# Two fused transformer blocks on one core: final norms placed by hand, the residual added by accumulating transfers, a two-part compression product

## The chip, the cores and the metric

The kernel runs on one core of one Trainium2 chip, as one launch. The metric is the device time of one execution in microseconds (us). The number given for the kernel before is the median of three runs; a fourth run was profiled, and every row of a trace below comes from that one execution. A change counts as measurable here from about 0.2% on.

## The reference, cut to what matters

Two blocks over 512 tokens of width 2048, in float32. The first is a gated block (linear recurrence beside latent attention), which the change doesn't touch. Of the second, this is what it touches:

```python
def compress(kv, pe, w1, w2):            # keys and values for the compressed attention
    ch = kv.reshape(b, s // 16, 16, g, d)                  # b=1, s=512, g=4, d=64
    blocks = jnp.concatenate([ch[:, r:nc + r] for r in range(2)], axis=2)   # 32 long, stride 16
    blocks = blocks + pe[None, None, :, None, :]
    hid = jax.nn.silu(jnp.einsum('bnlgd,lde->bnge', blocks, w1))
    return jnp.einsum('bnge,ef->bngf', hid, w2)

def second_block(x, p, ...):
    ...
    x = x + merged @ w_out                                              # x2 below
    x = x + jax.nn.sigmoid(x @ w_ple_gate) * (p @ w_ple)                # gated product
    return rms_norm_2(x, final_g)                                       # x * rsqrt(mean(x^2) + eps) * final_g
```

## The kernel before

**Precision.** TensorE's operands are float32 values split into two float32r parts, hi and lo (`split`: ScalarE rounds to hi, VectorE subtracts to get lo), and a product is three matmuls, hi·hi, hi·lo and lo·hi (`mm3`).

**Order.** The program is one stream. `spine` is a list of units, each with a weight tile (fetched on the SP queue, split ahead of use) and a generator of matmuls. Everything that isn't spine work is a generator in `sides`. After each step of a unit, `pump` advances those generators whose awaited tiles are known to be ready by `Clock`, a planner that adds up assumed durations for each engine and for transfers; `until` and `drain` advance them regardless, the one whose tiles are ready first going first. What comes out is a fixed order for each engine: an instruction that waits holds all that stand behind it on its engine. Intermediate tiles of 128x512 come from one pool of 78 slots (`slot`), and a transfer into a slot waits until the slot's last reader is done.

**Compression** (`compress`, once for keys, once for values, while the spine does the input product of the second block). For each of four groups `c`, VectorE adds the position term into `a`, a 128x(4x128) tile; ScalarE rounds it to `cAh`, VectorE subtracts to get `cAl`; then 8 matmuls of 128 columns go into `hid`, alternating between `cAh` and `cAl` with the same weights `w1`, whose 128 columns hold the hi and lo parts of 64 outputs. So there are 2 x 4 x 8 = 64 matmuls.

**The gate product** x2 @ w_ple_gate runs as Strassen's seven products on 256-token halves (`PROD`, in the order 1, 7, 6, 2, 5, 3, 4), for two pairs of 512-column quarters (p = 0, 1). The operand sums are the `F` tiles; those of products 5 and 3 are made by `late_forms` while the product of pair 0 runs. Output tile (b, c) is token block b (of 128 tokens) and column quarter c. Product 2 completes tiles (0, 2p) and (1, 2p), product 5 (2, 2p+1) and (3, 2p+1), product 3 (0, 2p+1) and (1, 2p+1), product 4 (2, 2p) and (3, 2p). So with p = 1, the last tile of blocks 0 and 1 comes from product 3, and that of blocks 2 and 3 from product 4, which is the last.

**The gated sum** (`gated`). `gate_load` brings two tiles from DRAM by POOL's queue: p @ w_ple (`plel`, stored early in the program) and x2 (`x3`, called x in the trace). Then ScalarE: tanh(src/2); VectorE (`stt`): t = (t + 1) * plel; VectorE (`stt`): x = 0.5 t + x; ScalarE: square of x with a row sum into `ssq`; and a multiplication by the norm's gain on VectorE for some tiles. The tiles of quarter c = 0, 1 get their gain later (`first_gains`).

**The end** (`last_product`, `finish`). The last product is cut by token block: block 2 first (tile j = 0, 512 columns), then block 3 in two halves of 256 columns (24 matmuls each). After each part its gated sum is emitted at once. `finish(b)` then sums the four row sums, takes the reciprocal root in nine small VectorE instructions, scales the four tiles (three or two on ScalarE, the rest on VectorE) and sends four transfers of 256 KB to the output, on SP, ACT, SP and POOL's queues. `finish(0)` and `finish(1)` wait as generators and are emitted, with the others, in `drain` after the last matmul.

Of the kernel before, what the change touches and what calls it, by code (L numbers as in the profile page):

```python
# [9 lines left out]
F32R = mybir.dt.float32r  # L10
I32 = mybir.dt.int32
AF = mybir.ActivationFunctionType
OP = mybir.AluOpType
# [3 lines left out]
D = 2048  # L17
# [226 lines left out]
def emit(ctx, tc, I, out):  # L244
    nc = tc.nc
    V, A, T, G, Q = nc.vector, nc.scalar, nc.tensor, nc.gpsimd, nc.sync
# [6 lines left out]
    clock = Clock()  # L253

    def slot(shape, name, dt=F32):
        return sp.tile(shape, dt, name=name, tag="s", padded_shape=None)
# [7 lines left out]
    def small(name, n=16):  # L264
        return mp.tile([128, n], F32, name=name, tag="m")
# [4 lines left out]
    def f(ap):  # L270
        return ap.bitcast(F32)
# [10 lines left out]
    def tt(o, a, b, op):  # L282
        V.tensor_tensor(o, a, b, op=op)  # L283
        clock.note("V", 0.07 + size(o) * 1.04e-3, [o], [a, b])
# [16 lines left out]
    def stt(o, a, s, b, op0, op1, **k):  # L301
        V.scalar_tensor_tensor(o, a, s, b, op0=op0, op1=op1, **k)  # L302
        clock.note("V", 0.07 + per_lane(s) + size(o) * 1.04e-3, [o, *k.values()], [a, s, b])
# [9 lines left out]
    def act(o, a, fn=AF.Identity, **k):  # L313
        A.activation(o, a, fn, **k)  # L314
        n = sum(isinstance(x, bass.AP) for x in k.values())
        clock.note("A", (0.05 if psum(a) else 0.095) + 0.093 * n + size(a) * 0.835e-3,
                   [o] + ([k["accum_out"]] if "accum_out" in k else []), [a, *k.values()])

    def mm(o, l, r, start, stop_, on=False):

        T.matmul(o, l, r, start=start, stop=stop_, skip_group_check=on)  # L321
        clock.note("PE", max(0.107, size(r) * (0.419e-3 if r.dtype == F32R else 1.67e-3)), [o], [l, r])
# [5 lines left out]
    def dma(q, o, a):  # L328
        {"Q": Q, "A": A, "G": G}[q].dma_start(o, a)
        clock.dma(q, o, a)  # L330
# [9 lines left out]
    def mm3(o, lh, ll, rh, rl, start=False, stop_=False, on=False):  # L340
        mm(o, lh, rh, start, False, on)
        mm(o, lh, rl, False, False, on)
        mm(o, ll, rh, False, stop_, on)
# [57 lines left out]
    sides = Sides(clock, WIDTH)  # L401
# [38 lines left out]
    def ple_unit(c):  # L440
        def mmf(hi, lo):
            for b in range(TB):
                ps = bank("pple")
                t = slice(b * 128, (b + 1) * 128)
                for kk in range(2):
                    mm3(ps, pTh[kk][:, t], pTl[kk][:, t], hi[:, kk, :], lo[:, kk, :], kk == 0, kk == 1)
                squares((XK + (KT,) * 16)[4 * c + b])
                o = slot([128, 512], "pleo")
                act(o, ps, AF.Copy)
                stores.append((ple_d[b][c], o))  # L450
                first_group(4 * c + b - RB)
                yield

        return Unit(block("w_ple_2", 0, 2, (c * 512, (c + 1) * 512)), (2, 512), mmf)
# [342 lines left out]
    kl0, kl1, _ = PARTS[0][-1]  # L797
# [616 lines left out]
    oa_d = [dram(f"oa{i}") for i in range(8)]  # L1414
    sg_d = [dram(f"sg{i}") for i in range(32)]
    c1 = 0.7978845608028654
    done = {"oa": [], "ob": [], "sg": [], "x2": 0, "c22": 0}

    def gelu2_gen(x, **k):

# [162 lines left out]
    def compress(kind):  # L1583
# [4 lines left out]
        w1 = []  # L1588
        w1v = w1_.rearrange("(l q) d e -> (q d) l e", q=2)
        w1r = []  # L1590
        for half in range(2):
            w = slot([128, 8, 64], "w1r")
# [5 lines left out]
        for g in range(4):  # L1598
            e = slot([128, 264], "E")
            V.memset(e[:, 256:264], 0.0)  # L1600
            src = kc_[kind, g // 2][(g % 2) * 64:(g % 2 + 1) * 64]
# [9 lines left out]
        for q in range(4):  # L1611
            w = slot([128, 4, 128], "w1s", F32R)
            src = w1r[q // 2][:, (q % 2) * 4:(q % 2) * 4 + 4, :]
# [8 lines left out]
        hid = bank("phid")  # L1622
        for c in range(4):
            a = slot([128, 4, 128], "cA")
            o, r0 = c // 2, (c % 2) * 4
            for g in range(4):
                ev = E[g].rearrange("p (n r) -> p r n", r=8)
                tt(a[:, :, g * 32:(g + 1) * 32], ev[:, r0:r0 + 4, o:o + 32],
                   pec[:, 4 * c:4 * c + 4, None].to_broadcast([128, 4, 32]), OP.add)
            ah, al = slot([128, 4, 128], "cAh", F32R), slot([128, 4, 128], "cAl", F32R)  # L1630
            yield [a]
            act(ah, a, AF.Copy)
            yield [ah]
            tt(al, a, f(ah), OP.subtract)
            yield [al]
            for l in range(4):
                mm(hid[:, :128], w1[c][:, l, :], ah[:, l, :], c == 0 and l == 0, False)
                mm(hid[:, :128], w1[c][:, l, :], al[:, l, :], False, c == 3 and l == 3)
        yield [hid]
        hs, th = slot([64, 128], "hs"), slot([64, 128], "th")  # L1640
        act(th, hid[64:128, :128], AF.Copy)
        yield [th]
        tt(hs, hid[:64, :128], th, OP.add)
        yield [hs]
        act(th, hs, AF.Tanh, scale=0.5)
        yield [th]
# [287 lines left out]
    sg = {}  # L1934
# [62 lines left out]
    x2_d = dram("x2t", (128, TB, D))  # L1997
    x2r, F = {}, {}
# [120 lines left out]
    x3, pl_, acc, tmp, part = {}, {}, {}, {}, {}  # L2119

    def gate_load(b, c):
        x3[b, c] = slot([128, 512], "x3")
        pl_[b, c] = slot([128, 512], "plel")
        dma("G", pl_[b, c], ple_d[b][c])
        dma("G", x3[b, c], x2_d[:, b, c * 512:(c + 1) * 512])

    def gated(b, c, src, s=slice(0, 512), end=None):

        yield [src, x3[b, c], pl_[b, c]]
        x = x3[b, c][:, s]  # L2130
        t = slot([128, 512], "tgate")[:, s]
        act(t, src, AF.Tanh, scale=0.5)
        yield [t]
        stt(t, t, 1.0, pl_[b, c][:, s], OP.add, OP.mult)
        stt(x, t, 0.5, x, OP.mult, OP.add)
        if end is not None:
            stt(t, x, 1.0, x, OP.mult, OP.mult, accum_out=end)
            return
        yield [x]
        act(t, x, AF.Square, accum_out=ssq[:, b, c:c + 1])  # L2140
        if c > 1 and (b < 2 or c == 3):
            tt(x, x, pl_["fg", c], OP.mult)
        pl_.pop((b, c))
        nsum[b] += 1
        if b < 2 and nsum[b] == 4:
            yield [ssq]
            sides.spawn(finish(b, ()))
        if b > 1 and nsum[b] == 3:
            sides.spawn(part_gen(b))

# [2 lines left out]
    def first_gains():  # L2153
        for c in range(2):
            for b in range(TB):
                yield [x3[b, c]]
                tt(x3[b, c], x3[b, c], pl_["fg", c], OP.mult)
        done["gains"] = True
# [39 lines left out]
    def from_4(j, c):  # L2198
        t, ps = tmp.pop(("w", j)), acc.pop(("e", j))
        yield [t, ps]  # L2200
        tt(t, ps, t, OP.subtract)
        yield from gated(2 + j, c, t)
# [59 lines left out]
        return [mk(u) for u in range(4)]  # L2262

    def last_product(u, ws):
        def part_(j, ks, s, end):
            ps = acc["e", j][:, s]
            for k in ks:
                hi, lo = ws[k // 2]
                w, t = F["4", k], slice(j * 128, (j + 1) * 128)
                mm3(ps, w[:, 0, t], w[:, 1, t], hi[:, k % 2, s], lo[:, k % 2, s], False, k == 7, True)  # L2270
                yield
            if end is not None:
                x = tmp["w", j][:, s]
                tt(x, ps, x, OP.subtract)
                for _ in gated(2 + j, 2, x, s, end):
                    pass

        e0 = small("sqe")
        yield from part_(0, (2 * u, 2 * u + 1), slice(0, 512), e0[:, 0:1] if u == 3 else None)
        if u == 3:  # L2280
            sides.spawn(finish(2, (e0[:, 0:1],)))
            e1, e2 = small("sqe"), small("sqe")
            yield from part_(1, range(8), slice(0, 256), e1[:, 0:1])
            yield from part_(1, range(8), slice(256, 512), e2[:, 0:1])
            sides.spawn(finish(3, (e1[:, 0:1], e2[:, 0:1])))

    def part_gen(b):
        yield [ssq]
# [2 lines left out]
        tt(p[:, 0:1], p[:, 0:1], ssq[:, b, 3:4], OP.add)  # L2291
        ts(p[:, 0:1], p[:, 0:1], 1.0 / D, EPS, OP.mult, OP.add)

    def finish(b, sums):

        while "gains" not in done:
            yield
        yield
        if sums:
            ms = part[b]  # L2300
            for o in sums:
                stt(ms[:, 0:1], o, 1.0 / D, ms[:, 0:1], OP.mult, OP.add)
        else:
            ms = part[b] = small("part")
            reduce(ms[:, 0:1], ssq[:, b, :], OP.add)
            ts(ms[:, 0:1], ms[:, 0:1], 1.0 / D, EPS, OP.mult, OP.add)
        r = rsqrt1(ms)
        yield
        for n, c in enumerate((2, 3, 1, 0)):
            y = x3[b, c]  # L2310
            if sums and c == 2:
                stt(y, y, r, pl_["fg", c], OP.mult, OP.mult)
            elif n < 3:
                act(y, y, AF.Identity, scale=r)
            else:
                ts(y, y, r, None, OP.mult)
            dma("QAQG"[n], out[0, b * 128:(b + 1) * 128, c * 512:(c + 1) * 512], y)

    def rsqrt1(ms):

# [115 lines left out]
```

## Time and profile before

| | |
|---|---|
| median of 3 runs | 2384.18 us (2383.25 to 2385.69) |
| the profiled execution | 2384.71 us, its span in the trace 2382.8 us |
| TensorE (PE) busy | 2339.3 us, 98% of the span, 11323 matmuls |
| VectorE (DVE) busy | 1534.0 us, 64% |
| ScalarE (ACT) busy | 974.7 us, 41% |
| GpSimd (POOL) busy | 291.9 us, 12% |
| mean granted TensorE clock | 0.995 of full speed |
| moved by transfers | 383.10 MB, mean 161 GB/s |

Times in rows are in us from the start of the span, durations in us unless marked ns. PE's weight loads (PEld) overlap its matmuls, and a matmul's printed duration is longer than the distance to the next one, since they are pipelined: the pace is read from the starts. On DVE and ACT too the next instruction can start some tenths of a us before the printed end of the one before. "Idle before" is the time that an engine waited, with what released it.

### The profile page before, as it was taken

Reading aid. Unit: us, or ns where it says so; the run is one execution under the profiler, and the core shown is the slowest. Engines: PE = TensorE matmul, PEld = TensorE weight load, DVE = VectorE, ACT = ScalarE, POOL = GpSimd, SP = SyncE. Lnnn points to the kernel's source line nnn. Section 1 sums busy time; section 2 is a strip of 40 time slices with the busy share of each in tenths; the row PEclk is TensorE's granted clock in tenths of the full one; section 3 lists DMA queues with packets and bytes.
Section 4 is the critical chain, followed back from the end, with each engine's and each line's share of the span. In section 5 each row is a group of like instructions: output and inputs, shape, how many; then the busy total and the mean of one; then the engine's idle time right before and its main releaser. Section 6 shows DMA issues by size and latency. Waiting matters only on the chain.

```text
span 2382.8 us, 30848 instructions
## 1 busy us (share of the span) xinstructions
PE 2339.3 (98%) x11323; PEld 1960.3 (82%) x11323; DVE 1534.0 (64%) x2918; ACT 974.7 (41%) x1791; POOL 291.9 (12%) x432
## 2 busy tenths in 40 slices
PE   8999999999999999999999999999999999999996
PEld 6778889888888988888888888888888888888785
DVE  6777988788866357558888437877233445333777
ACT  6423265655533343335444224544223222222554
POOL 0000030342212002000010100000111200110120
PEclk9999999999999999999999999999999999999998
DMA  9986732333355354624444634444545633444684
GB/s 344 350 271 239 256 129 72 124 122 105 111 177 185 97 160 139 185 89 124 130 127 142 172 98 124 125 110 128 144 148 178 216 111 111 140 134 133 234 300 150
DMA packets 124167, 383.10 MB, mean 161 GB/s; under 512 B 16542, under 2 KB 16836, under 8 KB 123504
## 3 DMA queue, kind: packets, MB, share of 16 engines
q1 hardware_dynamic: 94896, 273.41, 35.1%
q0 software_dynamic: 28256, 106.58, 15.0%
q8 instruction: 89, 1.46, 0.2%
q10 hardware_dynamic: 864, 1.14, 0.1%
q14 instruction: 62, 0.51, 0.1%
HBM read 343.32 MB, written 71.30 MB: 174 GB/s over the span
## 4 chain that ended last, share of the span: by engine, by line
PE 58%; DVE 3%; issue 1%; ACT 1%; DMA 1%; POOL 0%; ACTq 0%; DVEq 0%; POOLq 0%
PE pch L321 46%; PE pgb L321 2%; PE pO L321 2%; PE psc L321 2%; PE pge L321 2%; PE pPT L325 1%; DVE wlo L283 1%; PE pgc L321 1%; PE pga L321 0%; ACT whi L314 0%; DVE cA L283 0%; PE pcs L321 0%; PE px L325 0%; DMA w1r<-in_cmp_w_v_dram 0%; DVE vx L302 0%
## 5 line engine op out<-in xcount | busy, mean ns | idle before, releaser
L283 DVE TENSOR_TENSOR wlo<-wraw,whi 128x1024 fp32r<-128x1024 f32 (+5 forms) x421 | 497.5, 1182 | 191.7 <-ACT whi L314 189.5
L314 ACT ACTIVATE whi<-wraw 128x1024 fp32r<-128x1024 f32 (+5 forms) x423 | 425.1, 1013 | 318.8 <-PE pch L321 118.9
L321 PE MATMUL pch<-h2h,whi 128*128 128x512 f32 x1216 | 483.2, 397 | 0.0
L321 PE MATMUL pch<-h2h,wlo 128*128 128x512 f32 x1216 | 474.9, 391 | 0.0
L321 PE MATMUL pch<-h2l,whi 128*128 128x512 f32 x1216 | 474.5, 390 | 0.0
L321 PEld LDWEIGHTS pch<-h2h,wlo 128*128 128x128 f32 x1216 | 228.2, 188 | 48.9
L321 PEld LDWEIGHTS pch<-h2l,whi 128*128 128x128 f32 x1216 | 228.8, 188 | 40.7
L321 PEld LDWEIGHTS pch<-h2h,whi 128*128 128x128 f32 x1216 | 228.6, 188 | 41.0
L314 ACT ACTIVATE P<-psc,sm 128x512 f32<-128x512 f32 (+3 forms) x160 | 83.7, 527 | 134.2 <-DVE sm L306 103.9
L321 PE MATMUL pp<-hh,whi 128*128 128x512 f32 x320 | 126.1, 394 | 0.2 <-DVE acc L283 0.2
L321 PE MATMUL pp<-hh,wlo 128*128 128x512 f32 x320 | 124.7, 390 | 0.0
L321 PE MATMUL pp<-hl,whi 128*128 128x512 f32 x320 | 124.6, 389 | 0.0
L321 PE MATMUL pch<-mgh,whi 128*128 128x512 f32 x256 | 101.1, 395 | 0.0
L321 PE MATMUL pch<-mgh,wlo 128*128 128x512 f32 x256 | 99.9, 390 | 0.0
L321 PE MATMUL pch<-mgl,whi 128*128 128x512 f32 x256 | 99.6, 389 | 0.0
L321 PE MATMUL pch<-oh,whi 128*128 128x512 f32 x256 | 99.6, 389 | 0.0
L321 PE MATMUL pch<-ol,whi 128*128 128x512 f32 x256 | 99.6, 389 | 0.0
L321 PE MATMUL pch<-oh,wlo 128*128 128x512 f32 x256 | 99.6, 389 | 0.0
L283 DVE TENSOR_TENSOR mg<-pch,R 128x512 f32<-128x512 f32 x32 | 22.1, 690 | 116.4 <-PE pch L321 116.4
L314 ACT ACTIVATE PTh<-pPT 128x512 fp32r<-128x512 f32 (+1 forms) x120 | 59.6, 529 | 90.7 <-PE pPT L325 88.3
L306 DVE TENSOR_REDUCE sm<-psc 128x1 f32<-128x512 f32 (+3 forms) x160 | 78.6, 491 | 5.5
L283 DVE TENSOR_TENSOR PTl<-pPT,PTh 128x512 fp32r<-128x512 f32 (+1 forms) x120 | 68.1, 594 | 9.8 <-ACT PTh L314 9.6
(538 smaller groups left out, 4755.6 us busy)
## 6 DMA issues: line engine op xcount, KB each, us to landing
wraw<-in_w_in_dram SPq DMA_DIRECT2D x199, 512.0 KB, 3.6
wada<-in_w_mod_dram SPq DMA_DIRECT2D x128, 256.0 KB, 5.4
wraw<-in_w_out_dram SPq DMA_DIRECT2D x64, 512.0 KB, 3.5
wgate<-in_w_gate_dram SPq DMA_DIRECT2D x64, 256.0 KB, 4.8
wraw<-in_w_ple_gate_dram SPq DMA_DIRECT2D x24, 512.0 KB, 4.2
ws0x<-in_w_ple_gate_dram POOLq DMA_DIRECT2D x16, 512.0 KB, 7.8
ws1x<-in_w_ple_gate_dram POOLq DMA_DIRECT2D x16, 512.0 KB, 6.2
sg<-mg POOLq DMA_DIRECT2D x32, 256.0 KB, 2.6
```

Source lines behind the costliest of these rows:

```text
L283: V.tensor_tensor(o, a, b, op=op)
L306: V.tensor_reduce(o, a, AX.X, op, **k)
L314: A.activation(o, a, fn, **k)
L321: T.matmul(o, l, r, start=start, stop=stop_, skip_group_check=on)
L325: T.transpose(o, a, i)
```

## The change

It does three things.

1. Compression: `cAh` and `cAl` of two of the four rows of `a` now lie side by side in one tile `cA2`, so that one matmul of 256 columns takes both parts: 32 matmuls instead of 64. The rounding and the subtraction go in halves of 256 columns (two of each per group instead of one), and at the end the two halves of `hid` are added with one more ScalarE copy and two more VectorE additions.
2. The residual: p @ w_ple is stored with a factor 0.5. For 14 of the 16 tiles x2 is no longer loaded ahead; VectorE makes (t + 1) * plel in place, and a transfer from DRAM on POOL's queue with an accumulate adds x2 to it. The square, and all behind it, waits for that transfer. Tiles (2, 2) and (3, 2) keep the load of x2 and an addition on VectorE.
3. The end: the last product has no halves any more (24 matmuls of 512 columns for block 3). Before the gated sum of block 2 is emitted, `until` emits `finish(0)` and `finish(1)` to their end; `finish(2)` is emitted behind block 2's gated sum, ahead of block 3's matmuls in the program, and block 3's sum and `finish(3)` follow.

```diff
@@ -446,7 +446,7 @@
                     mm3(ps, pTh[kk][:, t], pTl[kk][:, t], hi[:, kk, :], lo[:, kk, :], kk == 0, kk == 1)
                 squares((XK + (KT,) * 16)[4 * c + b])
                 o = slot([128, 512], "pleo")
-                act(o, ps, AF.Copy)
+                act(o, ps, AF.Copy, scale=0.5)
                 stores.append((ple_d[b][c], o))
                 first_group(4 * c + b - RB)
                 yield
@@ -1414,7 +1414,7 @@
     oa_d = [dram(f"oa{i}") for i in range(8)]
     sg_d = [dram(f"sg{i}") for i in range(32)]
     c1 = 0.7978845608028654
-    done = {"oa": [], "ob": [], "sg": [], "x2": 0, "c22": 0}
+    done = {"oa": [], "ob": [], "sg": [], "x2": 0, "c22": 0, "out": 0}
 
     def gelu2_gen(x, **k):
 
@@ -1627,20 +1627,25 @@
                 ev = E[g].rearrange("p (n r) -> p r n", r=8)
                 tt(a[:, :, g * 32:(g + 1) * 32], ev[:, r0:r0 + 4, o:o + 32],
                    pec[:, 4 * c:4 * c + 4, None].to_broadcast([128, 4, 32]), OP.add)
-            ah, al = slot([128, 4, 128], "cAh", F32R), slot([128, 4, 128], "cAl", F32R)
-            yield [a]
-            act(ah, a, AF.Copy)
-            yield [ah]
-            tt(al, a, f(ah), OP.subtract)
-            yield [al]
-            for l in range(4):
-                mm(hid[:, :128], w1[c][:, l, :], ah[:, l, :], c == 0 and l == 0, False)
-                mm(hid[:, :128], w1[c][:, l, :], al[:, l, :], False, c == 3 and l == 3)
+            for half in range(2):
+                w = slot([128, 2, 2, 128], "cA2", F32R)
+                src = a[:, 2 * half:2 * half + 2]
+                yield [a]
+                act(w[:, :, 0], src, AF.Copy)
+                yield [w]
+                tt(w[:, :, 1], src, f(w[:, :, 0]), OP.subtract)
+                yield [w]
+                for l in range(2):
+                    n = 4 * c + 2 * half + l
+                    mm(hid[:, :256], w1[c][:, 2 * half + l, :], w[:, l].rearrange("p h n -> p (h n)"), n == 0, n == 15)
         yield [hid]
         hs, th = slot([64, 128], "hs"), slot([64, 128], "th")
         act(th, hid[64:128, :128], AF.Copy)
-        yield [th]
-        tt(hs, hid[:64, :128], th, OP.add)
+        act(hs, hid[64:128, 128:256], AF.Copy)
+        yield [hs]
+        tt(th, hid[:64, :128], th, OP.add)
+        tt(hs, hid[:64, 128:256], hs, OP.add)
+        tt(hs, hs, th, OP.add)
         yield [hs]
         act(th, hs, AF.Tanh, scale=0.5)
         yield [th]
@@ -2119,32 +2124,39 @@
     x3, pl_, acc, tmp, part = {}, {}, {}, {}, {}
 
     def gate_load(b, c):
-        x3[b, c] = slot([128, 512], "x3")
+
         pl_[b, c] = slot([128, 512], "plel")
         dma("G", pl_[b, c], ple_d[b][c])
-        dma("G", x3[b, c], x2_d[:, b, c * 512:(c + 1) * 512])
-
-    def gated(b, c, src, s=slice(0, 512), end=None):
-
-        yield [src, x3[b, c], pl_[b, c]]
-        x = x3[b, c][:, s]
-        t = slot([128, 512], "tgate")[:, s]
+        if b > 1 and c == 2:
+            x3[b, c] = slot([128, 512], "x3")
+            dma("G", x3[b, c], x2_d[:, b, c * 512:(c + 1) * 512])
+
+    def gated(b, c, src):
+
+        yield [src, pl_[b, c]]
+        t, p = slot([128, 512], "tgate"), pl_.pop((b, c))
         act(t, src, AF.Tanh, scale=0.5)
         yield [t]
-        stt(t, t, 1.0, pl_[b, c][:, s], OP.add, OP.mult)
-        stt(x, t, 0.5, x, OP.mult, OP.add)
-        if end is not None:
-            stt(t, x, 1.0, x, OP.mult, OP.mult, accum_out=end)
+        if b > 1 and c == 2:
+            x = x3[b, c]
+            stt(t, t, 1.0, p, OP.add, OP.mult)
+            tt(x, t, x, OP.add)
+            e = small("sqe")[:, 0:1]
+            stt(t, x, 1.0, x, OP.mult, OP.mult, accum_out=e)
+            sides.spawn(finish(b, e))
             return
+        x = x3[b, c] = p
+        stt(x, t, 1.0, p, OP.add, OP.mult)
+        G.dma_start(x, x2_d[:, b, c * 512:(c + 1) * 512], accum_op=OP.add, max_dma_last_dim=2048)
+        clock.dma("G", x, x)
         yield [x]
         act(t, x, AF.Square, accum_out=ssq[:, b, c:c + 1])
-        if c > 1 and (b < 2 or c == 3):
+        if c > 1:
             tt(x, x, pl_["fg", c], OP.mult)
-        pl_.pop((b, c))
         nsum[b] += 1
         if b < 2 and nsum[b] == 4:
             yield [ssq]
-            sides.spawn(finish(b, ()))
+            sides.spawn(finish(b))
         if b > 1 and nsum[b] == 3:
             sides.spawn(part_gen(b))
 
@@ -2153,6 +2165,8 @@
     def first_gains():
         for c in range(2):
             for b in range(TB):
+                while (b, c) not in x3:
+                    yield
                 yield [x3[b, c]]
                 tt(x3[b, c], x3[b, c], pl_["fg", c], OP.mult)
         done["gains"] = True
@@ -2262,27 +2276,18 @@
         return [mk(u) for u in range(4)]
 
     def last_product(u, ws):
-        def part_(j, ks, s, end):
-            ps = acc["e", j][:, s]
+        for j, ks in ((0, (2 * u, 2 * u + 1)), (1, range(8) if u == 3 else ())):
+            t = slice(j * 128, (j + 1) * 128)
             for k in ks:
                 hi, lo = ws[k // 2]
-                w, t = F["4", k], slice(j * 128, (j + 1) * 128)
-                mm3(ps, w[:, 0, t], w[:, 1, t], hi[:, k % 2, s], lo[:, k % 2, s], False, k == 7, True)
+                w = F["4", k]
+                mm3(acc["e", j], w[:, 0, t], w[:, 1, t], hi[:, k % 2, :], lo[:, k % 2, :], False, k == 7, True)
                 yield
-            if end is not None:
-                x = tmp["w", j][:, s]
-                tt(x, ps, x, OP.subtract)
-                for _ in gated(2 + j, 2, x, s, end):
+            if u == 3:
+                sides.until(lambda: done["out"] >= 2 + j)
+                for _ in from_4(j, 2):
                     pass
-
-        e0 = small("sqe")
-        yield from part_(0, (2 * u, 2 * u + 1), slice(0, 512), e0[:, 0:1] if u == 3 else None)
-        if u == 3:
-            sides.spawn(finish(2, (e0[:, 0:1],)))
-            e1, e2 = small("sqe"), small("sqe")
-            yield from part_(1, range(8), slice(0, 256), e1[:, 0:1])
-            yield from part_(1, range(8), slice(256, 512), e2[:, 0:1])
-            sides.spawn(finish(3, (e1[:, 0:1], e2[:, 0:1])))
+                sides.until(lambda: done["out"] == 3 + j)
 
     def part_gen(b):
         yield [ssq]
@@ -2291,30 +2296,30 @@
         tt(p[:, 0:1], p[:, 0:1], ssq[:, b, 3:4], OP.add)
         ts(p[:, 0:1], p[:, 0:1], 1.0 / D, EPS, OP.mult, OP.add)
 
-    def finish(b, sums):
+    def finish(b, e=None):
 
         while "gains" not in done:
             yield
-        yield
-        if sums:
+        if e is not None:
             ms = part[b]
-            for o in sums:
-                stt(ms[:, 0:1], o, 1.0 / D, ms[:, 0:1], OP.mult, OP.add)
+            stt(ms[:, 0:1], e, 1.0 / D, ms[:, 0:1], OP.mult, OP.add)
         else:
             ms = part[b] = small("part")
             reduce(ms[:, 0:1], ssq[:, b, :], OP.add)
             ts(ms[:, 0:1], ms[:, 0:1], 1.0 / D, EPS, OP.mult, OP.add)
         r = rsqrt1(ms)
-        yield
+        if e is None:
+            yield [ms]
         for n, c in enumerate((2, 3, 1, 0)):
             y = x3[b, c]
-            if sums and c == 2:
+            if e is not None and c == 2:
                 stt(y, y, r, pl_["fg", c], OP.mult, OP.mult)
             elif n < 3:
                 act(y, y, AF.Identity, scale=r)
             else:
                 ts(y, y, r, None, OP.mult)
             dma("QAQG"[n], out[0, b * 128:(b + 1) * 128, c * 512:(c + 1) * 512], y)
+        done["out"] += 1
 
     def rsqrt1(ms):
 
```

## Rows read from the trace of the kernel before

**Rows 1.** Engines' busy time by stretch, with the granted clock and the transfers' share.

```profile
2232.00:2257.00 25.00, 22.57 (x101) 18.36 (x99) 20.96 (x36) 14.26 (x25) 2.14 (x4) 0.99 0.68 231
...
2362.70:2382.80 20.10, 0.00 (x0) 0.00 (x0) 11.35 (x54) 7.41 (x11) 2.18 (x4) 0.58 0.56 209
```

**Rows 2.** What PE waited for, whole span: us in total, times, longest.

```profile
PE pgb L321 <- ACT F L314: 2.4, 1, 2.4
PE pge L321 <- DVE wq L283: 1.7, 1, 1.7
...
PE phid L321 <- DVE cAl L283: 1.6, 2, 0.9
```

**Rows 3.** PE's instructions in order during the compression: start, us, engine, line, operation.

```profile
960.17 0.33 PE L321 MATMUL phid<-cAl,w1s 128*128 128x128 f32 x1 [0.87 <-DVE cAl L283]
...
965.83 0.22 PE L321 MATMUL phid<-cAh,w1s 128*128 128x128 f32 x1
...
966.96 0.40 PE L321 MATMUL pch<-h2l,whi 128*128 128x512 f32 x1
```

**Rows 4.** PE's instructions in order in the last product's 256-column part.

```profile
2355.00 0.40 PE L321 MATMUL pge<-whi,F 128*128 128x256 f32 x2
...
2355.36 0.40 PE L321 MATMUL pge<-whi,F 128*128 128x256 f32 x2
```

**Rows 5.** Chain that ended last, in order of time, around PE's stall.

```profile
2256.89 3.75 PE pgb L321 x9
2260.64 10.88 PE pgc L321 x48
```

**Rows 6.** VectorE in order, in the stretch before that stall.

```profile
2249.57 0.69 DVE L302 SCALAR_TENSOR_TENSOR tgate<-tgate,plel 128x512 f32<-128x512 f32 x1
...
2250.91 1.22 DVE L283 TENSOR_TENSOR wlo<-wraw,whi 128x1024 fp32r<-128x1024 f32 x1
```

**Rows 7.** Transfers by line, whole span: count, size, median us from issue to landing.

```profile
x1p<-x1p POOLq DMA_DIRECT2D x16, 256.0 KB, 3.6
...
x<-x2t POOLq DMA_DIRECT2D x16, 256.0 KB, 6.8
```

**Rows 8.** The accumulating transfers of 512 KB (line 2107): time to landing.

```profile
DMA to landing us min/median/max: 5.1/8.4/24.2
```

**Rows 9.** Tile x2t from 2190 on: POOL's issues (ns) and times to landing.

```profile
L329 POOL DMA_DIRECT2D x<-x2t x16: 538/538/643, 2205.6 to 2304.7; - x16
...
DMA to landing us min/median/max: 2.7/6.6/9.7
```

**Rows 10.** VectorE in order at the end.

```profile
2350.56 0.69 DVE L302 SCALAR_TENSOR_TENSOR tgate<-tgate,plel 128x512 f32<-128x512 f32 x1
...
2356.66 0.08 DVE L302 DVE_READ_ACCUMULATOR tgate<-x 128x1 f32 x1
...
2364.50 0.15 DVE L302 SCALAR_TENSOR_TENSOR part<-sqe,part 128x1 f32<-128x1 f32 x1
...
2366.47 0.75 DVE L302 SCALAR_TENSOR_TENSOR x<-x,part,fg 128x512 f32<-128x512 f32 x1
...
2367.53 0.15 DVE L306 TENSOR_REDUCE part<-ssq 128x1 f32<-128x4 f32 x1
...
2369.69 0.49 DVE L292 TENSOR_SCALAR x<-x,part 128x512 f32<-128x512 f32 x1
```

**Rows 11.** ScalarE in order at the end.

```profile
2353.93 0.63 ACT L314 ACTIVATE tgate<-wq 128x512 f32<-128x512 f32 x1 [3.51 <-DVE wq L283]
...
2354.99 0.19 ACT L314 ACTIVATION_READ_ACCUMULATOR tgate<-x 128x1 f32 x1
...
2367.65 0.72 ACT L314 ACTIVATE x<-x,part 128x512 f32<-128x512 f32 x1 [0.46 <-ACT x L314]
...
2375.47 1.33 ACT L314 ACTIVATE x<-x,part 128x512 f32<-128x512 f32 x2 [1.33 <-DVE part L302]
...
2377.22 0.72 ACT L314 ACTIVATE x<-x,part 128x512 f32<-128x512 f32 x1 [0.42 <-ACT x L314]
```


## The prediction

> **What bounds the kernel now.** I read the waits of PE first. The whole list is short: PE waits for something that this change touches only three times in earnest, 2.4 us for ScalarE's copy of an F tile, 1.7 us for VectorE at the border of the two 256-column halves, and 1.6 us in two pieces for the compression's lo part [rows 2]. So nearly everywhere the time is the sum of PE's own instructions, and cheaper VectorE work is worth nothing except where PE stalls on it. The busy times by stretch show the two exceptions. Around the 2.4 us stall VectorE is busy for 20.96 of 25 us, PE for 22.57. And in the last 20.1 us PE does nothing, while VectorE is busy for 11.35 us and ScalarE for 7.41 [rows 1]: that is the end, four norms one behind the other. The reader should take from this that the change has three places, each priced in its own way: PE's pace, one stall, and a chain of VectorE and ScalarE.
>
> **Compression: PE's pace.** Eight 128-column matmuls begin at 965.83, and the second spine matmul behind them at 966.96 [rows 3]. One spine matmul of 512 columns takes 10.88/48 = 0.227 us [rows 5], so a group of eight costs 1.13 - 0.23 = 0.90 us, and eight groups 7.2 us. With 256 columns three matmuls go from 2355.00 to 2355.36 [rows 4], 0.12 us each, so the new 32 cost 3.84 us: 3.4 us less. If each of the 16 new pairs pays 0.06 us at its border to the spine's matmuls, 1 us of that is lost, 2.4 us. I take 3.1. The waits for the lo part, 1.6 us before, could go, or come twice as often, since there are twice as many groups: plus or minus 1.6. I leave them as they are. The extra halves on ScalarE and VectorE and the additions at the end I cost at nothing: what they delay is the compressed keys, which the program uses some units later, while spine matmuls go on. Without that cover they would cost their own length: eight more halves of what is done already, at the 0.15 us that an instruction of one column takes [rows 10], 1.2 us, and four additions of 128 columns between 0.15 and 0.69, so some 2 us.
>
> **The sum with x2, and the stall in pair 0.** For 14 tiles one VectorE instruction goes. One pair of them, tgate and x, takes from 2249.57 to 2250.91, so 0.67 us each [rows 6]. Where PE doesn't wait for VectorE this is worth nothing. In the stretch before the stall two go, 1.34 us. The stall costs more than its 2.43 us: the nine matmuls behind it take 3.75 us where nine at 0.227 take 2.04, 1.7 us more [rows 5]. Gone altogether it gives 4.1 us. Shortened by 1.34 us it gives 1.3, or 3.05 if the remaining 1.1 us no longer slows PE; the 0.87 us wait in the compression is followed by no slower matmuls [rows 3]. Against it stands the new wait. ScalarE's square needs the accumulated tile, and behind it on ScalarE stand copies of F tiles and of weights, for which PE waits. Tile (0, 0) is ready for its transfer at about 2250.2 and (1, 0) 0.67 us later. If a transfer lands L us after its issue, an F copy (256 columns, an estimated 0.4 after the 0.63 of 512 in [rows 11]) behind both squares (0.7 for the last) ends at 2250.2 + 0.67 + L + 1.1 = 2252 + L, where before PE went on at 2256.89 [rows 5]: a loss of L - 4.9. If the planner puts the copies ahead of the squares, nothing is lost. So this place lies between -4.1 and +3.5 (L = 8.4, below); I take -1.0.
>
> **How long an accumulating transfer takes** the trace doesn't show for 256 KB into SBUF. Near rows: plain 256 KB transfers on the same queue take 2.7 us at the fastest [rows 9], 3.6 in the median for an earlier tile, and 6.8 for the loads of x2 themselves, which come bunched [rows 7]. Accumulates of 512 KB take 5.1 at the fastest and 8.4 in the median [rows 8]. I take L = 3.8 at the end, where no weight is being fetched any more, nearer to the 3.6 of the plain ones, with 2.7 and 6.8 as ends. POOL's issue (0.54) is in L; nothing else stands on POOL's queue there, since its last load is issued at 2304.7 [rows 9]. The Trainium skill (DMA: Bandwidth & Descriptors, section Anatomy of one DMA) gives a transfer of GpSimd's queue a fixed cost of about 2 us plus its bytes at 436 GB/s, 2.6 us for 256 KB as an estimate. By that rule the addition is 2 us dearer as a transfer than as the VectorE instruction wherever somebody waits for it; the end below would be 1.2 us earlier than with my 3.8, and the sum -6.05. The 2.7 us of [rows 9] agree with it, the medians don't.
>
> **The end.** Now the halves are gone, so block 3's 24 matmuls end 24 x 0.227 = 5.45 us after block 2's, without the 1.7 us of waiting. Block 2's difference is taken just before the tanh at 2353.93 [rows 11], its product ends some 0.7 before that, so PE ends at about 2358.6. But nobody waits for them. In program order finish(0) and finish(1) now stand ahead of block 2's gated sum on VectorE and ScalarE. I follow this on the old clock. The products of (0, 3) and (1, 3) with plel start at 2350.56 and 2351.23 [rows 10]; the first transfer goes out at 2351.25 and lands at 2355.05, the second 0.65 later. The square with its sum takes 0.7 (tanh and square end 1.25 after 2353.93 [rows 11]), to 2355.75; the gain 0.65, as one of [rows 6]; finish(0)'s small instructions 2.16 (2367.53 to 2369.69 [rows 10]), to 2358.55; the gain of (1, 3) and finish(1) 2.8, to 2361.35. ScalarE's three scalings and one issue take 2.47 (2375.47 to 2377.94), two take 1.90 (2366.47 to 2368.37) [rows 10, 11]. So ScalarE has block 0 done at 2361.0 and block 1 at 2363.8, and only then comes the tanh of (2, 2). From tanh to the row sum is 2.81 (2353.93 to 2356.74), from there to the scaling 1.97 (2364.50 to 2366.47): 2368.6 [rows 10, 11]. Two scalings, 2370.5, hide VectorE's difference for (3, 2); then 4.78 again, 2375.3, and two scalings, 2377.2. Before, the last scaling ended at 2377.94 and the span 4.86 later [rows 1, 11]. So the new end is 2382.05, a gain of 0.75 us only: the norms of blocks 0 and 1 are moved from behind PE's end to the front, but the transfer and the serial order eat what is saved. Per us of L the end moves by one: from -1.85 (L = 2.7) to +2.25 (L = 6.8). The factor 0.5 in the store costs nothing: it is an argument of an instruction that is there anyhow.
>
> **Sum.** -3.1 - 1.0 - 0.75 = -4.85 us. The profiled execution took 2384.71 us with a span of 2382.8, 0.5 us above the median of the runs. The same difference from that median gives 2384.18 - 4.85 = 2379.3 us, 0.20% less, just at what a measurement of this kernel can tell from no change (0.2%, 4.8 us).
>
> **The rivals.**
> *The stall goes altogether.* VectorE's 1.34 us and fewer slots held (x2 no longer has 14 of its own) let the F tiles be ready in time: -3.1 - 4.1, and the end with L = 2.7, -1.85: 9.05 us less, 2375.1. For it: VectorE is that stretch's limit [rows 1]. Against it: ScalarE gets 14 waits that it didn't have. 20%.
> *Compression saves little.* The 16 smaller groups catch VectorE late more often, twice the 1.6 us, and pay at each border: -2.4 + 1.6 = -0.8, with the other terms -2.55, 2381.6. For it: two of eight groups were late already [rows 2]. Against it: the planner waits for both parts now. 17%.
> *The transfer is late, and ScalarE stands.* One mechanism at two places, F copies behind squares in pair 0 and the end's start. With L for both the sum is -3.1 + (L - 4.9) + (L - 4.55), which is zero at L = 6.3; with the 8.4 of [rows 8] it is +4.25, 2388.4, slower. For it: loads of x2 took 6.8 in the median [rows 7]. Against it: at the end the queues are empty, and in pair 0 the planner allows for a delay. 13%.
> *As summed.* 50%, with its own range of 2376.5 to 2382.
>
> **Numbers.** The forecast is 2379.3. The range takes in the first rival with some 1.5 us to spare (2373.5) and the beginning of the third (2384.5). Faster by over 0.2% (under 2379.4): half of the summed case, the first rival and little of the second, 0.50. Slower by over 0.2%: the third beyond L = 8.4, 0.07. Within: 0.43.
>
> **What would show it.** Right: the phid matmuls are 32 with 0.12 us from start to start; the accumulates land in 3 to 5 us; PE's stall in pair 0 of 1 to 2 us; PE's last matmul 5.45 us behind block 2's, yet a tail of some 23 us behind it; in the end ScalarE's tanh of (2, 2) waiting behind six scalings. Wrong: new waits of PE for ScalarE with squares behind accumulates; landings of over 6 us; new stalls between 981 and 2200, where the planner's order is now another and I count none.

## The result, and the profile after

The changed kernel takes 2400.43 us in the median of four runs (2399.99 to 2401.18), the kernel before 2384.66 (2383.25 to 2385.69): 1.0068 times, with a 95% interval of 1.0055 to 1.0080. The forecast was 2379.3, the range ended at 2384.5; the mechanism of the third rival, a late transfer on which ScalarE stands, happened, at about four times the price that I gave it (4.25 us in all, by its sum; 15.8 measured). The profiled execution took 2401.18 us, its span 2399.2.

**Where the time went.** Two marks in the trace cut the span into stages that nothing else shifts: POOL's last store of `sv`, just ahead of the compression, and its last store of x2, at the start of the gate product. The rows of the two tiles end with the first and the last start:

```profile
L329 POOL DMA_DIRECT2D sv<-svo x8: 539/548/579, 918.4 to 946.7; - x8
```

```profile
L329 POOL DMA_DIRECT2D x2t<-x2o x16: 709/723/740, 2032.2 to 2202.7; - x16
```

and before:

```profile
L329 POOL DMA_DIRECT2D sv<-svo x8: 542/550/579, 916.7 to 945.0; - x8
```

```profile
L329 POOL DMA_DIRECT2D x2t<-x2o x16: 712/724/740, 2033.9 to 2204.4; - x16
```

From the one to the other it is 2202.7 - 946.7 = 1256.0 us; before it was 2204.4 - 945.0 = 1259.4. So the compression gave 3.4 us. What precedes it differs by 1.7 us (946.7 against 945.0), though nothing was changed there but a factor; over the twelve kernels of this case that mark lies anywhere from 943.1 to 947.9. From the last store of x2 to the end it is 196.5 us against 178.4: 18.1 us were lost in the gate product and the end.

The longest waits of PE in the gate product, as in [rows 2] (us in total, times, longest). The last is the stall of before, 2.6 us now and 2.4 then; the other three are new:

```profile
PE pge L321 <- DVE wlo L283: 3.8, 5, 1.5
PE pge L321 <- ACT whi L314: 3.1, 3, 1.5
PE pgb L321 <- ACT whi L314: 2.7, 1, 2.7
PE pgb L321 <- ACT F L314: 2.6, 1, 2.6
```

And these are two of the longest sums between 2203 us and the end, on VectorE and ScalarE:

```profile
DVE wlo L283 <- ACT whi L314: 42.9, 25, 9.1
ACT tgate L314 <- DMA plel<-x2t: 38.6, 12, 7.1
```

The row to read is the second: ScalarE's square (it writes the `tgate` tile) waits for the accumulated tile 12 times, 38.6 us together. The first is in part its echo: VectorE waits for the weights' hi parts that stand behind those squares. It waited for them before as well, but never for long:

```profile
DVE wlo L283 <- ACT whi L314: 29.3, 23, 3.4
```

How one of them becomes a stall of PE is seen by following it through three engines. ScalarE:

```profile
2276.20 1.04 ACT L314 ACTIVATE whi<-wraw 128x1024 fp32r<-128x1024 f32 x1
2284.32 0.63 ACT L314 ACTIVATE tgate<-plel 128x512 f32<-128x512 f32 x1 [7.08 <-DMA plel<-x2t]
...
2286.50 0.63 ACT L314 ACTIVATE tgate<-plel 128x512 f32<-128x512 f32 x1 [1.45 <-DMA plel<-x2t]
...
2287.13 1.99 ACT L314 ACTIVATE whi<-wraw 128x1024 fp32r<-128x1024 f32 x2
```

VectorE, whose `wlo` needs the `whi` of ScalarE, idle for 9.1 us:

```profile
2277.88 1.22 DVE L283 TENSOR_TENSOR wlo<-wraw,whi 128x1024 fp32r<-128x1024 f32 x1
2288.20 1.23 DVE L283 TENSOR_TENSOR wlo<-wraw,whi 128x1024 fp32r<-128x1024 f32 x1 [9.10 <-ACT whi L314]
```

and PE, which needs both:

```profile
2288.22 0.49 PE L321 MATMUL pgb<-whi,F 128*128 128x512 f32 x1 [2.65 <-ACT whi L314]
2289.48 0.50 PE L321 MATMUL pgb<-wlo,F 128*128 128x512 f32 x1 [0.77 <-DVE wlo L283]
```

Between 2277 and 2284 ScalarE does nothing at all; two copies of weights stand behind the two squares that wait. PE uses up the weights that were split ahead and then waits. A stretch with the columns of [rows 1] shows the second price too:

```profile
2260.00:2300.00 40.00, 34.28 (x133) 26.88 (x133) 21.79 (x31) 19.12 (x35) 10.83 (x16) 0.91 0.74 215
```

In 2260 to 2300 PE is busy for 34.28 us with 133 matmuls, which at 0.227 us are 30.2: after its waits the granted clock is 0.91 on the mean of that stretch, that is, part of it is spent at 1.2 GHz.

Where the time is lost shows in PE's rows at the starts of the products. One of 48 matmuls took 10.88 us before [rows 5], except where the stall is:

```profile
2258.50 0.63 PE L321 MATMUL pgc<-whi,F 128*128 128x512 f32 x1
...
2271.75 0.50 PE L321 MATMUL pge<-whi,F 128*128 128x512 f32 x1 [1.54 <-ACT whi L314]
...
2301.87 0.39 PE L321 MATMUL pge<-whi,F 128*128 128x512 f32 x1
```

With the start at 2288.22 above, the three products right behind the stall take 13.25, 16.47 and 13.65 us, 10.7 more than three times 10.88. The product with the stall itself took 14.7 us (2243.77 to 2258.50) against 15.0 before (2245.46 to 2260.48). Of the rest of the loss some 6 us lie in the last product and some 2 in those between.

How long the accumulating transfers take (duration of POOL's issue in ns; us from issue to landing):

```profile
L2150 POOL DMA_DIRECT2D plel<-x2t x14: 862/882/1187, 2247.7 to 2367.2; - x14
...
DMA to landing us min/median/max: 4.0/6.1/8.2
```

### The profile page after: what moved, and what is told of

The parts are those of the page before. It is cut to its first block, busy times and chain, and to the rows that moved or that the text cites. A ratio compares the mean times of both kernels' runs of the same rounds, so it can differ in the third digit from the quotient of the medians.

```text
span 2399.2 us, 30735 instructions
## 1 busy us (share of the span) xinstructions
PE 2341.8 (98%) x11267; PEld 1956.8 (82%) x11267; DVE 1523.8 (64%) x2910; ACT 974.1 (41%) x1800; POOL 297.3 (12%) x432
## 3 DMA queue, kind: packets, MB, share of 16 engines
q0 software_dynamic: 29152, 106.58, 15.6%
## 4 chain that ended last, share of the span: by engine, by line
PE 81%; issue 9%; DVE 4%; DMA 3%; POOL 1%; ACT 1%; SPq 0%; POOLq 0%; DVEq 0%; ACTq 0%
PE pch L321 47%; PE ppan L321 9%; PE pp L321 9%; PE po L321 6%; PE psc L321 3%; PE pO L321 3%; PE pPT L325 2%; PE pearly L321 1%; DVE wlo L283 1%; DMA wada<-in_w_mod_dram 1%; DMA xT<-in_xT_dram 0%; POOL plel L2150 0%; PE pmod L535 0%; POOL plel L329 0%; DMA w1r<-in_cmp_w_v_dram 0%
```

## The experiments

Each ratio is to runs of the kernel before that were taken beside the kernel's own. "To x2" is the time from the last store of `sv` to the last store of x2, "gate and end" the time from there to the end of the span, both in the profiled execution, so from one execution of each kernel; differences of 1 or 2 us in the last column are read with that in mind.

| kernel | median us | ratio to before (95%) | to x2 | gate and end |
|---|---|---|---|---|
| before | 2384.4 to 2385.2 | 1 | 1259.4 | 178.4 |
| changed | 2400.4 | 1.0068 (1.0055 to 1.0080) | 1256.0 | 196.5 |
| compress_only | 2383.5 | 0.9996 (0.9987 to 1.0005) | 1255.6 | 180.0 |
| accumulate_only | 2406.7 | 1.0092 (1.0078 to 1.0106) | 1259.3 | 200.0 |
| end_only | 2383.2 | 0.9996 (0.9988 to 1.0005) | 1259.5 | 177.0 |
| no_accumulate | 2381.2 | 0.9984 (0.9975 to 0.9993) | 1256.0 | 178.4 |
| square_elsewhere | 2376.2 | 0.9971 (0.9961 to 0.9982) | 1256.2 | 172.8 |
| late_plain | 2388.8 | 1.0022 (1.0012 to 1.0033) | 1256.0 | 185.3 |
| due_later | 2382.8 | 0.9996 (0.9987 to 1.0005) | 1256.0 | 178.3 |
| due_55 | 2381.2 | 0.9985 (0.9976 to 0.9994) | 1255.6 | 176.8 |
| due_80 | 2381.7 | 0.9986 (0.9977 to 0.9995) | 1255.9 | 178.4 |
| one_norm_ahead | 2382.4 | 0.9992 (0.9984 to 1.0001) | 1255.6 | 180.0 |

The theory: an instruction of ScalarE that waits for a transfer, placed ahead of weight copies, is what costs; the transfers' traffic and the rest of the change don't. The rivals: the new order in the end, the new order that the planner makes everywhere, and the traffic.

### Each part alone, and all but the accumulate

**compress_only**: the kernel before with the first of the three parts (the diff's part in `compress`).

> Only the two-part compression product is changed. Theory (the loss is all in the wait for the accumulating transfers): 3.4 us less than before, 2381, since PE's instructions shrink by that much and nothing waits anew. Rival (the new order that the planner makes costs time by itself): no gain or a loss, 2384 to 2387.

Measured 2383.5. The 3.4 us are there up to the gate product (x2's last store at 2201.2, 945.6 the mark before), but the gate product and the end take 1.6 us longer, so that the sum is not distinguishable from before:

```profile
L329 POOL DMA_DIRECT2D x2t<-x2o x16: 712/724/740, 2030.7 to 2201.2; - x16
```

Most of the 1.6 us lie at the stall: in PE's waits it is 2.56 us (2.43 before), with one of 0.36 ahead of it, and the product that holds it takes 15.87 us instead of 15.02. So the total is where the rival put it, but not for its reason: from the last store of x2 on, all engines' instructions stand in the same order in this trace and in the one of before. What differs is when a weights' load is there for ScalarE, before:

```profile
2217.68 1.06 ACT L314 ACTIVATE whi<-wraw 128x1024 fp32r<-128x1024 f32 x1 [1.50 <-DMA wraw<-ws0y]
```

and here:

```profile
2215.54 1.06 ACT L314 ACTIVATE whi<-wraw 128x1024 fp32r<-128x1024 f32 x1 [2.84 <-DMA wraw<-ws0y]
```

Counted from the last store of x2, that copy comes 1.1 us later here, and so do the F copies at the stall. Why the load is later stays open.

**accumulate_only**: the kernel before with x2 added by transfers (`ple` stored with a factor 0.5), everything else as before. The lines that matter:

```diff
-        stt(t, t, 1.0, pl_[b, c][:, s], OP.add, OP.mult)
-        stt(x, t, 0.5, x, OP.mult, OP.add)
+        stt(x, t, 1.0, p, OP.add, OP.mult)
+        G.dma_start(x, x2_d[:, b, c * 512:(c + 1) * 512], accum_op=OP.add, max_dma_last_dim=2048)
+        clock.dma("G", x, x)
```

> Only the addition of x2 by accumulating transfers is changed; compression and end are as before. Theory (ScalarE stands at the squares, and copies of weights and F tiles stand behind them): the whole loss and more, 17 to 20 us over before, 2401 to 2404, with PE waiting for ScalarE and VectorE some 10 us in the gate product. Rival (the end's new order is what loses): within 3 us of before.

Measured 2406.7, more than the whole loss. The same rows as above, between 2203 us and the end:

```profile
DVE wlo L283 <- ACT whi L314: 44.7, 22, 10.7
ACT tgate L314 <- DMA plel<-x2t: 39.2, 11, 8.6
...
PE pge L321 <- ACT whi L314: 4.8, 3, 3.4
...
PE pge L321 <- DVE wq L283: 4.6, 1, 4.6
...
PE pgb L321 <- ACT whi L314: 3.3, 1, 3.3
```

It lost 21.8 us, more than the 17 to 20 expected: the end that was kept has its border between the halves, and PE's wait there grew from 1.7 us [rows 2] to 4.6.

**end_only**: the kernel before with the new `last_product` and `finish`, x2 loaded and added as before.

> Only the end is changed: no halves in the last product, the norms of blocks 0 and 1 emitted ahead of block 2's gated sum; x2 is loaded ahead as before. Theory: the squares wait for nothing, so by the prediction's own chain the end is some 3 us earlier, 2381. Rival (six scalings on ScalarE ahead of block 2's tanh cost more than the halves' stall): 2 to 5 us slower, 2386 to 2389.

Measured 2383.2; gate and end take 1.4 us less. The ratio's interval takes in 1, so the gain itself is not shown. The end is no loss; at most it is half of the 3 us that the chain of the prediction gives without a transfer in it.

**no_accumulate**: the changed kernel with `gate_load` and the two VectorE instructions as before.

> The changed kernel with the addition of x2 put back as it was (loaded ahead, added on VectorE); compression and end as changed. Theory: both other parts give what they are worth, 3.4 + 3 us less than before, 2378. Rival (the end loses): 2383 to 2386.

Measured 2381.2, 0.16% less than before, clear of 1, and 19 us less than the changed kernel; the theory's 2378 was not reached. These four put the loss on the accumulating transfers, and none of it on the end.

### Wait, traffic or the accumulate

**square_elsewhere**: the changed kernel; the square and the gain read another tile, so the norms leave x2 out. In the trace every engine's order is that of the changed kernel, but for one instruction on ScalarE and one on VectorE that stand one place earlier or later.

```diff
-        act(t, x, AF.Square, accum_out=ssq[:, b, c:c + 1])
+        act(t, t, AF.Square, accum_out=ssq[:, b, c:c + 1])
         if c > 1:
-            tt(x, x, pl_["fg", c], OP.mult)
+            tt(t, t, pl_["fg", c], OP.mult)
```

> The changed kernel, with the square (and the gain of c = 2, 3) taken of the tanh's tile instead of the accumulated tile, so no instruction of ScalarE or VectorE waits for the transfer before the final scaling; the norms leave x2 out. All transfers stay. Theory (the wait on ScalarE): ScalarE's idle time for these transfers, 38.6 us, goes, PE's new waits with it, 2380 to 2385. Rival (the transfers' traffic): 2395 or more.

Measured 2376.2, lower than expected. The transfers are all there and land in 6.1 us in the median, the weights' loads in 4.2. Of PE's waits in the gate product one kind is left:

```profile
PE pge L321 <- DVE wlo L283: 1.3, 2, 0.8
```

and the 2.4 us stall of [rows 2] is gone: in the chain that ended last products follow each other at 10.88 us (start, us, matmuls).

```profile
2232.11 10.88 PE pga L321 x48
2242.99 10.88 PE pgb L321 x48
2253.87 10.88 PE pgc L321 x48
```

So the traffic costs nothing here that can be seen. Without the waits, gate and end take 5.6 us less than before: 1.9 up to the end of block 2's product, since the stall is gone, and 3.7 behind it, where no square waits for a transfer. How much of that comes from the VectorE instruction less for each tile isn't shown: the end is another one too, and the squares here don't wait for any addition.

**late_plain**: the changed kernel with plain transfers.

```diff
-        G.dma_start(x, x2_d[...], accum_op=OP.add, max_dma_last_dim=2048)
+        G.dma_start(x, x2_d[...], max_dma_last_dim=2048)
```

> The changed kernel with plain transfers in place of the accumulating ones, at the same places and into the same tiles (the output then leaves the gated product out); every engine's order is the same. Theory (any transfer issued only after the product costs its landing time, the accumulate little): landings 5 to 6 us in the median, 2395 to 2400. Rival (the accumulate itself is what is slow): landings of 3.5 us, ScalarE's wait halved, 2388 or less.

Measured 2388.8, between the two. The issue on POOL and the landing are both shorter (ns min/median/max; us in the median):

```profile
L2150 POOL DMA_DIRECT2D plel<-x2t x14: 536/536/541, 2246.2 to 2355.5; - x14
```

```profile
plel<-x2t POOLq DMA_DIRECT2D x14, 256.0 KB, 3.7
```

```profile
ACT tgate L314 <- DMA plel<-x2t: 24.9, 10, 4.3
```

With the same order on every engine, 0.54 us to issue and 3.7 to land instead of 0.88 and 6.1. The theory's 5 to 6 us for any transfer fell, and the rival came close: it had 3.5 us to land, half of ScalarE's wait (it is 24.9 us against 38.6) and 2388 at most. Of the 18.1 us that gate and end lost, 11.2 go with the accumulate in place of a plain transfer (196.5 against 185.3), and 6.9 to the addition's being a transfer with somebody waiting for it (185.3 against 178.4).

### The same instructions, placed later

**due_later**, **due_55** and **due_80**: the changed kernel; only the planner's account of the transfer is corrected, by 3.5, 5.5 and 8.0 us.

```diff
         clock.dma("G", x, x)
+        clock.ready[x.tensor.name] += 3.5
         yield [x]
```

> The changed kernel, with the planner told that an accumulating transfer lands 3.5 us later than it assumes (some 6.8 us after its issue instead of 3.3), so that squares are placed later in ScalarE's order; the instructions are the same. Theory (squares stand on ScalarE ahead of weight and F copies): most of PE's waits for ScalarE and VectorE in the gate product go, some 12 to 17 us, 2384 to 2389. Rival (the transfers themselves slow the weights' loads): 2396 to 2401.

> As due_later, with 5.5 us added to the planner's landing time instead of 3.5 (8.8 us after the issue, above the 8.2 of the slowest accumulate seen in the changed kernel). Theory (what is left of PE's waits in due_later comes from squares still ahead of their transfers): ScalarE's waits for these transfers fall from 5.4 us to under 3, some 2 to 4 us less than due_later, 2379 to 2381. Rival (what is left has other causes, or late squares hold other work up): no less than due_later, 2382.5 or more.

> The same with 8.0 us added (11.3 us after the issue). Theory: as due_55, 2379 to 2381, since nobody needs a square before the end of its row of tiles. Rival (late squares bunch up and hold weight copies): 2 us or more over due_55.

Measured 2382.8, 2381.2 and 2381.7: the first lower than the theory's 2384 to 2389, the other two 0.2 and 0.7 us above its 2379 to 2381. One line that changes no instruction but their order takes 17.6 us off the changed kernel (18.2 in gate and end). What is left of the waits with 3.5 us:

```profile
ACT tgate L314 <- DMA plel<-x2t: 5.4, 4, 3.0
...
PE pge L321 <- DVE wlo L283: 4.1, 4, 1.9
```

and with 5.5 us:

```profile
PE pge L321 <- DVE wlo L283: 2.8, 4, 0.8
...
ACT tgate L314 <- DMA plel<-x2t: 2.3, 2, 1.9
```

That the range from 3.5 to 8.0 makes so little difference agrees with the theory; the last transfers' wait stays (in due_80 it is 5.3 us in two), since the end forces those squares out whatever the planner believes. due_55, due_80 and no_accumulate lie 0.15, 0.14 and 0.16% under the kernel before, clear of 1, less than the 0.2% that count here, and can't be told from each other.

**one_norm_ahead**: no_accumulate with only block 0's norm ahead of block 2's gated sum.

```diff
-                sides.until(lambda: done["out"] >= 2 + j)
+                sides.until(lambda: done["out"] >= 1 + 2 * j)
```

> The version without accumulating transfers, with only block 0's norm ahead of block 2's gated sum and block 1's behind it. Theory (block 2's tanh waits behind six scalings on ScalarE): 1.5 to 2.5 us less than that version, 2379. Rival (VectorE's instructions are the limit of the end, in whatever order): within 0.7 us of it, 2381.

Measured 2382.4; the theory gave 2379, so it fell; the rival's 0.7 us around 2381 was missed by as much again. VectorE's differences for blocks 2 and 3 in no_accumulate:

```profile
2356.27 0.69 DVE L283 TENSOR_TENSOR wq<-pge,wq 128x512 f32<-128x512 f32 x1
...
2363.86 0.68 DVE L283 TENSOR_TENSOR wq<-pge,wq 128x512 f32<-128x512 f32 x1
```

and those of blocks 2 and 3 here:

```profile
2358.88 0.68 DVE L283 TENSOR_TENSOR wq<-pge,wq 128x512 f32<-128x512 f32 x1
...
2365.88 0.68 DVE L283 TENSOR_TENSOR wq<-pge,wq 128x512 f32<-128x512 f32 x1
```

Block 3's follows block 2's after 7.00 us instead of 7.59, since the tanh has fewer scalings ahead of it. But from there to the end of the span it is 15.6 us instead of 13.6 (2381.5 and 2377.5): the scalings come back in block 3's own chain. I read it so that the end is bound by all the work that it holds, on VectorE and ScalarE, more than by its order; one pair of kernels doesn't show that.

## Why the prediction was wrong

**What bounds the kernel** was read rightly: PE's own instructions and one stall. What I drew from it, that a change on VectorE or ScalarE is worth nothing elsewhere, holds only for work that is taken away. A wait that is added can use up the slack anywhere, and I looked for it at one place.

**Compression: right.** Predicted 3.1 less, with 2.4 to 3.4; measured 3.4 up to the gate product. All 32 are there, and a pair of them that nothing holds up takes 0.23 us from its start to the next spine matmul, 0.12 each as in [rows 4]:

```profile
L321 PE MATMUL phid<-cA,w1s x32: 274/282/386, 961.8 to 988.9; 128*128 128x256 f32 x32
```

```profile
969.12 0.39 PE L321 MATMUL phid<-cA,w1s 128*128 128x256 f32 x2
969.35 0.40 PE L321 MATMUL pch<-h2h,whi 128*128 128x512 f32 x1
```

That the sum came out at the upper end is in part luck: PE's waits for VectorE there, which I left at their 1.6 us, fell to 0.9,

```profile
PE phid L321 <- DVE cA L283: 0.9, 1, 0.9
```

so the instructions gave some 2.7 of the 3.4 us. New stalls between 981 and 2200 us, a sign of being wrong, are not there: in that stretch PE waits for nobody in either trace. What I left out is that the gate product can give part of it back, 1.6 us in the one kernel that has this part alone.

**The sum with x2: the step that failed.** Its term, -1.0 with +3.5 as the worst, should have been about +18 (alone, in accumulate_only, some 22). I worked out the loss as L - 4.9 at pair 0's F copies alone, and wrote against the rival that the planner allows for a delay. It allows for 3.3 us by its account; the transfers took 6.1 in the median, 8.2 at most. At the F copies themselves nothing was lost: the product with the stall took 14.7 us, 15.0 before. The loss came behind it, at the copies of weights, which I named there but didn't price. The 14 squares come in pairs, one pair for each of seven products; six of the pairs stand ahead of copies of weights on ScalarE, and PE has those only a few us ahead. So the rival's price had to be asked for at each of them, not once, and it wasn't the same at each: the three products behind the stall lost 10.7 us, the last one some 6, the others some 2. The waits of ScalarE alone sum to 38.6 us, of which PE has seen 14.3 us as waits (all of its waits for ScalarE and VectorE in the gate product; before 2.4, and 1.7 at the border of the halves). Up to the end of block 2's product it lost 18.5 us; the 6.6 that the waits don't cover are, by the matmuls' starts, some 4 of matmuls 0.43 us apart at the lower clock and some 2 around the waits' ends. The point from which it decides, L = 6.3 in my sum, is wrong for the same reason: with L = 3.7 (late_plain) gate and end lose 6.9 already.

**L itself.** I took 3.8 at the end, nearer to plain transfers; there it was 4.2 (issue at 2365.20, square at 2369.41, below):

```profile
2365.20 0.89 POOL L2150 DMA_DIRECT2D plel<-x2t  x1 [5.80 <-DVE plel L302]
```

In the gate product it was the accumulate's own length that counted, and [rows 8] had warned of it; 6.1 lies within the bounds that I gave, 2.7 to 8.4. By the Trainium skill's rule (DMA: Bandwidth & Descriptors, section Anatomy of one DMA; about 2 us and the bytes at 436 GB/s) a transfer of this size takes an estimated 2.6 us; that is under every accumulate here, the fastest of which took 4.0. The Trainium skill (DMA: Bandwidth & Descriptors, section Rules for kernel authors) says that an accumulate reads its destination and writes it later; that would fit a longer landing than a plain transfer's, but no run here takes it apart.

**The end: right in size, for reasons that held in part.** Predicted 0.75 less. VectorE, ScalarE and PE's last matmul in the changed kernel:

```profile
2377.58 0.69 DVE L283 TENSOR_TENSOR wq<-pge,wq 128x512 f32<-128x512 f32 x1
2380.28 0.69 DVE L302 SCALAR_TENSOR_TENSOR tgate<-tgate,plel 128x512 f32<-128x512 f32 x1 [2.01 <-ACT tgate L314]
```

```profile
2369.41 0.63 ACT L314 ACTIVATE tgate<-plel 128x512 f32<-128x512 f32 x1 [3.42 <-DMA plel<-x2t]
...
2374.87 1.33 ACT L314 ACTIVATE plel<-plel,part 128x512 f32<-128x512 f32 x2 [2.79 <-DVE part L302]
...
2379.63 0.61 ACT L314 ACTIVATE tgate<-wq 128x512 f32<-128x512 f32 x1
```

```profile
2375.06 0.39 PE L321 MATMUL pge<-whi,F 128*128 128x512 f32 x1
```

PE ends at 2375.45, so block 2's product at 2375.45 - 5.45 = 2370.0, 29.2 us ahead of the end; before it was 2382.8 - 2353.2 = 29.6. The tanh of block 2 does wait behind six scalings (VectorE's difference is there at 2378.3, the tanh comes at 2379.63 and VectorE sits idle for it until 2380.28), as I had it. Taking three of them out of its way gave nothing, though, as one_norm_ahead shows, and with no transfer in the chain (end_only) the gain was 1.4 us at most where the chain gives 3.

**The rival that the stall goes altogether** happened too, where nothing hid it: in square_elsewhere and in the kernels with a later due time that stall of PE is not there any more. So the F tiles can be ready in time, if the squares are out of the way, which I doubted; whether VectorE's 1.34 us did it isn't shown.

**Chances.** 0.13 for a late transfer and 0.07 for slower than the 0.2% were too low: the rows gave no bound for how often the wait would be met, and I took one meeting as the worst.

## What to carry to other kernels

If a step is moved from an engine to a transfer, list every instruction that now waits for it, what stands behind each on its in-order engine, and count the meetings, not the one at the tightest place. If a planner orders the program, its account of the new operation is part of the change: here one number in it was worth 17.6 us, more than the whole change lost. And price the transfer by one of its own kind: an accumulating one isn't a plain one.

## What the runs showed of the hardware that was not expected

An accumulating transfer of 256 KB from DRAM into SBUF took 6.1 us from issue to landing in the median (4.0 to 8.2), a plain one at the same place in the same program 3.7. Its issue on POOL has a printed duration of 0.88 us against 0.54, but so have the plain loads issued between the accumulates (0.87), and issues that follow one another stand about 0.55 us apart in both kernels. The weights' loads on SP's queue did not slow down: 4.4 us in the median of 20 with the accumulates, 4.3 with the plain ones. The plain loads on POOL's own queue did: those of p @ w_ple landed after 6.6 us in the median, against 5.4, and the four of the norm's gain after 9.0, against 6.3.
